# Seven block products instead of eight for five column pairs of the second token half in an input projection

## The chip, the cores and the metric

The kernel runs as one program on one core of a Trainium2 chip. The metric is device time in microseconds (us), the median over runs; before the change three runs gave 2535.07, 2537.70 and 2538.64 us, median 2537.7. The engines are named as in the profile: PE does the matrix products (a "matmul" is one instruction with up to 512 moving columns), DVE elementwise work on vectors, ACT elementwise functions and copies, POOL small elementwise work and DMAs of its own queue; SP issues most DMAs. A *bank* is one 128x512 fp32 accumulator of PE.

## The reference

One layer over T = 2048 tokens with D = 1024 features, all in fp32: token mixing, cross-attention into 256 memory tokens, and a gated feed-forward net, each between two RMS norms. The part around the change is token mixing:

```python
u = rms_norm(h, g_mix_pre[l])
z = u @ w_in[l]                      # (2048 x 1024) @ (1024 x 2816)
qa, ka, va, qh, fh, ih, gh = jnp.split(z, IN_SPLITS, axis=-1)
ya = swa_with_sinks(qa, ka, va, sinks[l])     # 8 query heads, 2 key heads, chunk-banded
yh = hgrn2(qh, fh, ih, gh, lb, onorm)         # 4 heads of a gated recurrence
y = concat([ya, yh]) @ w_out[l]
h = h + rms_norm(y, g_mix_post[l])
```

The 2816 columns of z are 22 columns of 128, numbered 0 to 21: 0 to 3 are attention's queries, 4 its keys, 5 its values, 6 to 9 the recurrence's queries, 10 to 13 its forget gates f, 14 to 17 its inputs, 18 to 21 its output gates.

## The kernel before, in words

**Products.** fp32 is emulated: each operand is split into a high part (`hi`, written by ACT or POOL) and a low part (`lo` = raw − hi, written by DVE, line 1038), and each product is three matmuls, hi·hi, hi·lo and lo·hi (`mm3`, lines 156 to 158, for plain products; `products`, lines 1198 to 1200, for block products).

**Block products.** Large products are cut into 2x2 blocks on both operands. A step with four results needs eight block products plainly, or seven with sums of operands and of results (the Winograd form; `seven`, in the order 1, 5, 6, 3, 7, 2, 4). The operand that stays is called T (tokens; T[1], T[8], T[2], T[3] are raw blocks, T[5], T[7], T[6], T[4] sums), the one that is loaded per step S (weights; `streamed`). For the input projection one step is a pair of columns for 1024 tokens: each block product is 12 matmuls of 128x512, so 84 in seven products and 96 plainly. The results leave the banks by ACT copies (`part`, line 1213) and by `out`, which adds on DVE and then applies what the column needs: a split into halves for columns 0 to 4, a copy, or a tanh with a product. For a pair with an f column, `after` runs `decays`: Ln on ACT, two cumulative scans on DVE (line 794), exponentials.

**Two token halves.** `in_first` handles tokens 0 to 1023 for all 11 pairs (`ORDER`: (4,5), (0,1), (2,3), (10,6), (11,7), (12,8), (13,9), (14,15) to (20,21)). Pairs 0 and 1 start in plain forms while the first tokens come in, the others are steps in seven products. `phases` plans them: it has a list of steps, knows at which step each T tile is used first and last, and forms a T tile (`resident`: ACT high part, DVE low part, in two halves) when a slot's last user is past. There are 7 slots. Then `in_first` splits the second half's four raw token blocks into `u` tiles and does the first pair of the second half plainly, 96 matmuls.

**Columns as filler.** The other 20 columns of the second half are done one at a time by `in_cols`: two token blocks of 24 matmuls each into a `psg` bank, with weights split by POOL or ACT (`whi`) and DVE (`wlo`). `in_proj` is a generator, and `mix` takes one column from it at given places between the steps of attention: one ahead, one after each of the first 9 rounds (a round is one step of `swa` and one of `hgrn`), one after each of the 8 remaining steps of `swa`, and two around the first step of `fold` (the cross-attention's preparation).

**An attention step.** `swa` works by blocks of 128 tokens. `swa_front(n)` loads queries and keys, makes scores on PE (128x256, lines 859 and 860), reduces and exponentiates them (line 864 on DVE with a read of its accumulator, line 868 on ACT), makes the softmax's denominators with small operations on POOL and ACT (lines 871 to 874) and scales (line 879 on DVE). `swa_back(n)` transposes on PE (line 893), splits into `pth` (ACT, line 897) and `ptl` (DVE, line 898), multiplies by the values (lines 902 and 903) and writes the result to `ys` by ACT (line 904), once for each of two key heads. `ys` has one buffer. It holds a high and a low partial result in two halves of its partitions: SP stores the first half into `y_d` in DRAM, and POOL's DMA adds the second half to the same place (line 907):

```python
ys = ph.tile([P, 2, 512], F32, tag="ys", name=f"ys{n}")
...
self.store(dst, ys[0:64])
nc.gpsimd.dma_start(dst, ys[64:128], accum_op=ALU.add)
```

`hgrn_front` loads k, q, v, multiplies k and q by decays on POOL (lines 931, 943, 946) and makes products on PE. The order on every engine is fixed when the program is built: a scheduler places the instructions of the generators by its own estimate of time, so a column need not stand where `mix` took it.

Of the kernel before, what the change touches and what calls it, by code (L numbers as in the profile page):

```python
# [18 lines left out]
P = 128  # L19
T = 2048  # L20
# [28 lines left out]
class Layer:  # L49
# [146 lines left out]
    def mix(self):  # L196
        tc, I = self.tc, self.I
        kw = dict(reuse_waits="tile")
        with contextlib.ExitStack() as left:
# [18 lines left out]
            with tc.tile_pool(name="sw", bufs=1, side="right", **kw) as self.sw:  # L218
# [5 lines left out]
                for _ in range(NPB + 1):  # L224
                    next(swa)
                    next(hgrn)
                    next(cols)
# [207 lines left out]

    ORDER = [(4, 5), (0, 1), (2, 3)] + [(10 + h, 6 + h) for h in range(4)] + [(c, c + 1) for c in range(14, 22, 2)]
# [31 lines left out]
    def in_first(self):  # L468
# [63 lines left out]
        second = {}  # L532

        def fetch():
            for s in range(2):
                for q in range(2):
                    r = self.pair_tile().rearrange("p a d -> p (a d)")
                    self.load(r.rearrange("p (n c) -> p n c", n=4),
                              self.un_d[4 * s:4 * s + 4, q].rearrange("n p c -> p n c"))
                    second[q, s] = r.rearrange("p (m k c) -> p k m c", m=16, k=4)  # L540
                    yield

        beside = [(), (0,), (1, 2), (3,), (4,), (5,), (6,), (7,), (), (), (), ()]
        get = fetch()
        tokens = [[] for _ in range(len(self.ORDER) + 1)]
        blocks = [("s",) + self.in_block(*p, tokens[i], tokens[i + 1], beside[i + 1], get if i > 9 else (), i < 2,
                                         None if i else lambda: x_loads(0, (2, 3)))
                  for i, p in enumerate(self.ORDER)]

# [3 lines left out]
        phases = self.phases([(lambda i, j, a, n: raw[i, j][:, a:a + n, :], 4, blocks, None, {})], T)  # L553
# [46 lines left out]
        for _ in get:  # L600
            pass
        u = []
        for s in range(2):
            u.append([])
            for q in range(2):
# [18 lines left out]
        for s in range(2):  # L624
# [1238 lines left out]
```

## Time and profile before

| | |
|---|---|
| runs | 2535.07, 2537.70, 2538.64 us; median 2537.7 |
| profiled execution | 2533.9 us, of which the span 2532.2 us |
| PE | busy 2493.8 us of the span (98%) |
| DVE, ACT, POOL | busy 1749.1, 1240.7 and 365.4 us |
| first token half and first pair of the second | about 0 to 280 us |
| attention steps with columns | about 285 to 616 us |
| cross-attention, feed-forward | from there to the end |

In the groups of the profile a line reads: source line, engine, operation, what it writes and reads, shape, count, then busy time, mean ns of one, and the idle time just before these instructions with what released most of it. In the timelines a row reads start, duration, engine, line, operation, and in brackets the idle time before it with its releaser. A busy PE includes overlap of neighbouring matmuls.

### The profile page before, as it was taken

The numbers are of one execution on the slowest core, as the hardware profiler recorded it, in microseconds if no ns is written. First come the engines' busy times: TensorE is split into PE (matmuls) and PEld (weight loads), VectorE is DVE, ScalarE is ACT, GpSimd is POOL, SyncE is SP. The second block draws the span as 40 slices with busy tenths as digits, with TensorE's granted clock in tenths as the row PEclk, the third lists the DMA queues.
The fourth block names the chain that finished last, engine by engine and source line by source line (L and its number), as shares of the span: only waits on it lengthen the run. The fifth ranks groups of instructions, "written<-read, shape, count | busy, mean of one in ns | idle before, by whom it ended". The sixth has DMA issues, their size and how long they took to land.

```text
span 2532.2 us, 33939 instructions
## 1 busy us (share of the span) xinstructions
PE 2493.8 (98%) x11942; PEld 2084.7 (82%) x11942; DVE 1749.1 (69%) x2787; ACT 1240.7 (49%) x2582; POOL 365.4 (14%) x540
## 2 busy tenths in 40 slices
PE   9999999999999999999999999999999999999998
PEld 8778888888987788878878888888888888888886
DVE  8896477865556989988866655576566557574766
ACT  5463356654565576566753333353333335443543
POOL 4241244321400111112200000000000000000122
PEclk9999999999999999999999999999999999999999
DMA  7544877785887996858944322254354334565777
GB/s 221 158 158 164 239 198 178 223 270 135 278 298 266 302 335 194 255 175 255 339 164 169 136 76 93 78 196 154 129 208 167 117 127 156 177 184 110 231 169 156
DMA packets 313403, 483.56 MB, mean 191 GB/s; under 512 B 21904, under 2 KB 198032, under 8 KB 313232
## 3 DMA queue, kind: packets, MB, share of 16 engines
q1 hardware_dynamic: 304880, 455.17, 54.1%
q0 software_dynamic: 8352, 26.22, 6.1%
q8 instruction: 94, 1.54, 0.2%
q14 instruction: 77, 0.63, 0.1%
HBM read 305.15 MB, written 176.16 MB: 190 GB/s over the span
## 4 chain that ended last, share of the span: by engine, by line
PE 83%; DVE 5%; DMA 5%; issue 2%; ACT 2%; POOL 1%; SPq 1%; DVEq 0%; POOLq 0%; ACTq 0%
PE psm L1200 22%; PE psm L1198 22%; PE psm L1199 22%; PE psg L158 2%; PE psg L156 2%; PE psg L157 2%; DVE S L1038 1%; DMA y_d<-ys 1%; DVE T L1038 1%; DMA raw<-in_wo_x_dram 1%; DVE sum L1173 0%; DMA pair<-in_x_dram 0%; DMA out_s<-u 0%; SPq L75 0%; ACT junk L1569 0%
## 5 line engine op out<-in xcount | busy, mean ns | idle before, releaser
L1198 PE MATMUL psm<-T,S 128*128 128x512 f32 x2680 | 1034.4, 391 | 12.6 <-ACT part L1213 8.4
L1199 PE MATMUL psm<-T,S 128*128 128x512 f32 x2680 | 1042.6, 390 | 1.2 <-DVE T L1038 1.1
L1200 PE MATMUL psm<-T,S 128*128 128x512 f32 x2680 | 1030.0, 390 | 5.0 <-DVE S L1038 5.0
L1198 PEld LDWEIGHTS psm<-T,S 128*128 128x128 f32 x2680 | 503.1, 188 | 124.8 <-ACT part L1213 13.0
L1200 PEld LDWEIGHTS psm<-T,S 128*128 128x128 f32 x2680 | 503.4, 188 | 112.4 <-DVE S L1038 8.4
L1199 PEld LDWEIGHTS psm<-T,S 128*128 128x128 f32 x2680 | 503.5, 188 | 106.7 <-DVE T L1038 3.0
L1035 ACT ACTIVATE S<-sum 128x512 fp32r<-128x512 f32 (+1 forms) x370 | 224.1, 619 | 374.8 <-PE psm L1200 270.4
L1038 DVE TENSOR_TENSOR S<-sraw,S 128x512 fp32r<-128x512 f32 (+1 forms) x315 | 212.0, 679 | 236.9 <-ACT S L1035 233.7
L1213 ACT ACTIVATE part<-psm 128x512 f32<-128x512 f32 x285 | 168.6, 596 | 253.1 <-PE psm L1200 237.8
L1038 DVE TENSOR_TENSOR S<-sum,S 128x512 fp32r<-128x512 f32 (+1 forms) x388 | 258.0, 673 | 43.9 <-ACT S L1035 40.0
L1035 ACT ACTIVATE S<-sraw 128x512 fp32r<-128x512 f32 (+1 forms) x300 | 184.5, 618 | 110.7 <-PE psm L1200 108.7
L1602 POOL DMA_DIRECT2D y_d<-row x16 | 14.0, 872 | 1077.3 <-DVE row L1784 1015.3
L1038 DVE TENSOR_TENSOR T<-row,T 128x1024 fp32r<-128x1024 f32 (+1 forms) x112 | 130.8, 1183 | 28.3 <-ACT T L1035 26.4
L156 PE MATMUL psg<-u,whi 128*128 128x512 f32 x320 | 127.6, 399 | 0.7 <-DVE z L770 0.5
L157 PE MATMUL psg<-u,whi 128*128 128x512 f32 x320 | 127.3, 398 | 0.0
L158 PE MATMUL psg<-u,wlo 128*128 128x512 f32 x320 | 126.7, 397 | 0.0
L1569 ACT ACTIVATE junk<-row 128x512 f32<-128x512 f32 x160 | 99.6, 624 | 46.3 <-DVE row L1591 19.9
L1035 ACT ACTIVATE T<-row 128x1024 fp32r<-128x1024 f32 (+1 forms) x112 | 113.4, 1031 | 10.6 <-DMA row<-d_s 5.3
L1735 DVE TENSOR_TENSOR row<-psm,part 128x512 f32<-128x512 f32 x66 | 44.0, 687 | 71.3 <-PE psm L1200 71.3
L1038 DVE TENSOR_TENSOR wlo<-raw,whi 128x1024 fp32r<-128x1024 f32 x52 | 65.4, 1258 | 36.0 <-ACT whi L1035 30.9
L1784 DVE TENSOR_TENSOR row<-psm,part 128x512 f32<-128x512 f32 x72 | 49.1, 687 | 49.3 <-PE psm L1200 49.2
L1744 DVE TENSOR_TENSOR part<-psm,part 128x512 f32<-128x512 f32 x66 | 43.7, 687 | 52.2 <-PE psm L1200 52.2
(355 smaller groups left out, 3476.2 us busy)
## 6 DMA issues: line engine op xcount, KB each, us to landing
sraw<-in_w_gate_dram SPq DMA_DIRECT2D x44, 512.0 KB, 3.8
sraw<-in_w_up_dram SPq DMA_DIRECT2D x44, 512.0 KB, 3.6
hid_d<-row SPq DMA_DIRECT2D x44, 512.0 KB, 2.6
sraw<-hid_d SPq DMA_DIRECT2D x32, 512.0 KB, 4.6
sraw<-in_w_in_dram SPq DMA_DIRECT2D x48, 256.0 KB, 3.9
raw<-in_w_in_dram SPq DMA_DIRECT2D x20, 512.0 KB, 6.3
row<-in_w_down_dram SPq DMA_DIRECT2D x20, 512.0 KB, 7.3
row<-d_s SPq DMA_DIRECT2D x20, 512.0 KB, 8.4
```

The lines of the kernel that those rows point to most:

```text
L156: nc.tensor.matmul(ps, ah, bh, start=(i == 0), stop=False)
L157: nc.tensor.matmul(ps, ah, bl, start=False, stop=False)
L158: nc.tensor.matmul(ps, al, bh, start=False, stop=(i == n - 1))
L1035: self.nc.scalar.activation(hi, raw, AF.Copy)
L1038: self.nc.vector.tensor_tensor(lo, raw, f32(hi), ALU.subtract)
L1198: nc.tensor.matmul(ps, s[:, 0, k, :], t[:, 0, k, :], start=st, stop=False, **kw)
L1199: nc.tensor.matmul(ps, s[:, 0, k, :], t[:, 1, k, :], start=False, stop=False, **kw)
L1200: nc.tensor.matmul(ps, s[:, 1, k, :], t[:, 0, k, :], start=False, stop=sp, **kw)
L1213: nc.scalar.activation(t, ps, AF.Copy)
L1569: self.nc.scalar.activation(junk, a, AF.Square, scale=float(D) ** -0.5, accum_out=to)
L1735: nc.vector.tensor_tensor(d, a, c, ALU.add)
L1784: nc.vector.tensor_tensor(d, a, b, ALU.add)
```

## The change

The second half's first five pairs, (4,5), (0,1), (2,3), (10,6) and (11,7), become steps in seven products as well, as a second job in `phases`. Twelve columns are left for `in_proj`.

- `sums` loads the four raw token blocks of the second half and makes in place, on DVE, what T[7], T[5] and T[6] need, in six operations of 128x1024; T[4] is a difference of two of these, made on the way. T[3]'s block and, at the third pair, T[8]'s block are loaded again.
- The second job's T tiles take the slots of the first job's tiles of the same number (`where`), each when its last user is past.
- The four `u` tiles and the plain pair go. Of the second job's T tiles, T[1], T[2] and T[3] serve the columns, and T[8] is split anew.
- `in_block` takes the token half as an argument; its two-scan `decays` now runs for two pairs of the second half there instead of in `in_cols`.
- `mix` takes columns at 12 places: one ahead, one after rounds 1, 3, 5 and 7, one after each remaining step of `swa` but two, and one at `fold`.

```diff
-                for _ in range(NPB + 1):
+                for i in range(NPB + 1):
                     next(swa)
                     next(hgrn)
-                    next(cols)
+                    if i in (1, 3, 5, 7):
+                        next(cols)
...
-                    next(cols)
+                    if i not in (11, 14):
+                        next(cols)
...
+    MORE = 5
...
+        more = [("s",) + self.in_block(*p, 1, (), [], (), False, None) for p in self.ORDER[:self.MORE]]
+        second = {}
+
+        def fetched(q, s):
+            r = self.pair_tile().rearrange("p a d -> p (a d)")
+            self.load(r.rearrange("p (n c) -> p n c", n=4),
+                      self.un_d[4 * s:4 * s + 4, q].rearrange("n p c -> p n c"))
+            return r.rearrange("p (m k c) -> p k m c", m=16, k=4)
+
+        def sums():
+            for k, at in ((7, (1, 1)), (5, (0, 1)), (1, (0, 0)), (2, (1, 0))):
+                second[k] = fetched(*at)
+                yield
+            for d, a, b, op in ((7, 7, 5, ALU.subtract), (5, 5, 1, ALU.subtract), (6, 1, 7, ALU.add)):
+                if d == 6:
+                    second[6] = self.pair_tile().rearrange("p a d -> p (a d)").rearrange("p (m k c) -> p k m c",
+                                                                                         m=16, k=4)
+                for k in (0, 2):
+                    kk = slice(k, k + 2)
+                    nc.vector.tensor_tensor(second[d][:, kk], second[a][:, kk], second[b][:, kk], op)
+                    yield
+
+        def operand(i, j, a, n):
+            key = i if j is None else {(0, 0): 1, (1, 0): 2, (1, 1): 3}[i, j]
+            if key == 3 and not a:
+                second[3] = fetched(1, 1)
+            if key == 4:
+                return second[2][:, a:a + n], second[6][:, a:a + n]
+            return second[key][:, a:a + n]
+
+        def again():
+            second[8] = fetched(0, 1)
+            yield
...
+        phases = self.phases([(lambda i, j, a, n: raw[i, j][:, a:a + n, :], 4, blocks, None, {len(blocks) - 2: [sums]}),
+                              (operand, 4, more, True, {2: [again]})], T)
...
-        u = []
-        for s in range(2):
-            u.append([])
-            for q in range(2):
-                self._n += 1
-                t = self.big.tile([P, 2, 4, 512], F32R, tag="big", name=f"u1_{q}{s}")
-                r = second[q, s]
-                for k in (0, 2):
-                    self.split2(r[:, k:k + 2], *(t[:, e, k:k + 2].rearrange("p k (m c) -> p k m c", m=16)
+        T[8] = self.big.tile([P, 2, 4, 512], F32R, tag="big", name="u1_01")
+        for k in (0, 2):
+            self.split2(second[8][:, k:k + 2], *(T[8][:, e, k:k + 2].rearrange("p k (m c) -> p k m c", m=16)
                                                  for e in range(2)), "A")
-                u[s] += [(t[:, 0, k, :], t[:, 1, k, :]) for k in range(4)]
-
-        c0 = self.ORDER[0][0] * P
-
-        def load(t, j):
-            for i, c in enumerate(self.ORDER[0]):
-                self.load(t[:, :, i * P:(i + 1) * P], I["w_in"][c, :, 4 * j:4 * j + 4, :])
-
-        stream = self.streamed(load, 4, "p")
-        next(stream)
-        S = list(stream)
-        z, low = self.pair_tile(), self.pair_tile()
-        for s in range(2):
-            sl = slice(s * 512, (s + 1) * 512)
-            for i in range(2):
-                ps = self.bank("g")
-                self.mm3(ps, [((S[i + k // 4 * 2][:, 0, k % 4, :], S[i + k // 4 * 2][:, 1, k % 4, :]), u[s][k])
-                              for k in range(KT)])
-                if i:
-                    nc.scalar.activation(z[:, i, sl], ps, AF.Copy)
-                else:
-                    self.halves(c0, ps, z[:, 0, sl], low[:, 0, sl])
-        self.store_halves(c0, TB, z[:, 0, :], low[:, 0, :])
-        self.store(self.z_d[c0 + P:c0 + 2 * P, TB:2 * TB], z[:, 1, :])
-        return u
+        for p in (1, 2, 3):
+            T[p] = T[1, p, 0]
+        return [[(T[p][:, 0, k, :], T[p][:, 1, k, :]) for p in ps for k in range(4)] for ps in ((1, 2), (8, 3))]
...
-        for c in order[2:]:
+        for c in order[2 * self.MORE:]:
...
+                if first and queue[0][0]:
+                    free = next(s for s in slots if s[2] == where[queue[0][1]])
```

How the built program differs at three places. Names carry a running number; an "x2" means two such instructions in a row. Line numbers behind the change are 2 to 7 lower.

PE late in the attention stage. Before, in the middle of one step (`psh` and `vst` are products with the values, `psg` with `whi` and `wlo` a column):

```order
L156 MATMUL psg_6266<-u_00_2232,whi_6261 128x512
L902 MATMUL psh_5937<-pth_10_5924,vst_5427 128x512
L157 MATMUL psg_6266<-u_00_2232,whi_6261 128x512
L158 MATMUL psg_6266<-u_00_2232,wlo_6262 128x512
L156 MATMUL psg_6266<-u_10_2237,whi_6261 128x512
L157 MATMUL psg_6266<-u_10_2237,whi_6261 128x512
L158 MATMUL psg_6266<-u_10_2237,wlo_6262 128x512
L156 MATMUL psg_6266<-u_10_2237,whi_6261 128x512
L903 MATMUL psh_5937<-ptl_10_5925,vst_5427 128x512
L902 MATMUL psh_5937<-pth_11_5933,vst_5626 128x512
```

After, at the corresponding stretch (`pss` and `pst` on `ident` are the transposes of the probabilities):

```order
L896 MATMUL psh_5776<-ptl_11_5773,vst_5467 128x512
L886 MATMUL pst_5942<-ident,S_00_5669 128x128 x2
L886 MATMUL pst_5942<-ident,S_01_5679 128x128 x2
L886 MATMUL pss_5933<-ident,S_00_5669 128x128 x2
L886 MATMUL pss_5933<-ident,S_01_5679 128x128 x2
L895 MATMUL psh_5951<-pth_00_5938,vst_5467 128x512
L886 MATMUL pss_5957<-ident,S_10_5702 128x128 x2
L886 MATMUL pss_5957<-ident,S_11_5712 128x128 x2
L886 MATMUL pst_5966<-ident,S_10_5702 128x128 x2
L886 MATMUL pst_5966<-ident,S_11_5712 128x128 x2
L896 MATMUL psh_5951<-ptl_00_5939,vst_5467 128x512
L895 MATMUL psh_5951<-pth_01_5947,vst_5664 128x512
```

The column's matmuls are gone from between the products with the values. Behind the eleventh of the twelve columns, 208 rows in a row, from the last of `psg_6472` to the first of `psg_6554`, hold no column's matmul; before, the longest such run is 23 rows. Counted with repeats, the 208 rows hold 125 matmuls of 128x128, 80 of 128x256, 56 of 128x512 and 4 of 128x192.

POOL at the end of these steps. `y_d<-ys` is the adding DMA, `w_se` and `w_dn` are the denominators of later steps, `k` is what PE's last product ahead of the twelfth column reads. Before:

```order
L907 DMA y_d<-ys_5695 64x2x512
L871 TENSOR_TENSOR w_se_5883<-sink,w_mn_5861 128x4
L874 TENSOR_TENSOR w_dn_5886<-w_den_5862,w_se_5883 128x4
L1037 TENSOR_SCALAR whi_6370<-raw_6368 128x1024
L871 TENSOR_TENSOR w_se_6047<-sink,w_mn_6025 128x4
L874 TENSOR_TENSOR w_dn_6050<-w_den_6026,w_se_6047 128x4
L907 DMA y_d<-ys_5894 64x2x512
L871 TENSOR_TENSOR w_se_6080<-sink,w_mn_6058 128x4
L874 TENSOR_TENSOR w_dn_6083<-w_den_6059,w_se_6080 128x4
L946 TENSOR_TENSOR k_6321<-k_6321,G_563 128x4x64
L907 DMA y_d<-ys_6091 64x2x512
```

After:

```order
L900 DMA y_d<-ys_5932 64x2x512
L864 TENSOR_TENSOR w_se_6060<-sink,w_mn_6038 128x4
L867 TENSOR_TENSOR w_dn_6030<-w_den_6006,w_se_6027 128x4
L867 TENSOR_TENSOR w_dn_6063<-w_den_6039,w_se_6060 128x4
L864 TENSOR_TENSOR w_se_6226<-sink,w_mn_6204 128x4
L900 DMA y_d<-ys_6071 64x2x512
L864 TENSOR_TENSOR w_se_6259<-sink,w_mn_6237 128x4
L867 TENSOR_TENSOR w_dn_6229<-w_den_6205,w_se_6226 128x4
L867 TENSOR_TENSOR w_dn_6262<-w_den_6238,w_se_6259 128x4
L900 DMA y_d<-ys_6270 64x2x512
L939 TENSOR_TENSOR k_6500<-k_6500,G_563 128x4x64
```

The splits `whi` of the columns' weights are gone from between, and `k` now stands directly behind the adding DMA of the last of these steps instead of ahead of it.

DVE where attention begins. `pair` here is the f pair's result and its scans, `wlo` the low part of a column's weights. Before:

```order
L1038 TENSOR_TENSOR S_2267<-sraw_2255,S_2267 128x512
L1038 TENSOR_TENSOR u_11_2247<-pair_2230,u_11_2247 128x1024 x2
L707 SCALAR_TENSOR_TENSOR pair_2169<-th_2190,pair_2169 128x512
L707 SCALAR_TENSOR_TENSOR pair_2169<-th_2210,pair_2169 128x512
L707 SCALAR_TENSOR_TENSOR pair_2169<-th_2225,psm_2096 128x512
L642 SCALAR_TENSOR_TENSOR pair_2271<-psm_2272,pair_2270 128x512
L1038 TENSOR_TENSOR wlo_2419<-raw_2416,whi_2418 128x1024
L1038 TENSOR_TENSOR wlo_2599<-raw_2596,whi_2598 128x1024
```

After:

```order
L687 TENSOR_TENSOR pair_2948<-psm_2867,part_2902 128x512
L807 SCALAR_TENSOR_TENSOR pair_2802<-pair_2802,pair_2887 128x1024
L687 TENSOR_TENSOR pair_2948<-psm_2984,part_2880 128x512
L700 SCALAR_TENSOR_TENSOR pair_2948<-th_2972,pair_2948 128x512
L700 SCALAR_TENSOR_TENSOR pair_2948<-th_3012,psm_2867 128x512
L787 SCALAR_TENSOR_TENSOR pair_3015<-reset,pair_3015 128x512 x2
L1031 TENSOR_TENSOR wlo_3078<-raw_3075,whi_3077 128x1024
L793 TENSOR_TENSOR pair_3015<-pair_3015,d_mid_3019 128x1024
```

Ahead of the first column's `wlo` there now stand the last f pair's sums and products and two scans (`pair_3015<-reset,pair_3015`).

More of the change, by code (lines that the diff above doesn't have):

```diff
@@ L648, in store_halves, with in_block @@
             self.store(dst[e, r:r + P, t0:t0 + t.shape[1]], t)
-    def in_block(self, ca, cb, x, ahead, beside, get, plain, between):
+    def in_block(self, ca, cb, b, x, ahead, beside, plain, between):
         nc, w = self.nc, self.I["w_in"]
@@ L662, in stream, with out @@
         def stream(kind):
-            for _ in range(3):
-                next(iter(get), None)
             return self.streamed(load, 4, kind)
-        def out(i, j, a, b):
+        def out(i, j, a, o):
             c0 = (ca, cb)[i] * P
@@ L1062, in split @@
         def split(a, b, t, o):
+            if type(t) is tuple:
+                t, o = t
             if o is not None:
                 nc.vector.tensor_tensor(t, t, o, ALU.add if key == 6 else ALU.subtract)
[L1065 removed]
+            hi, lo = dst[:, 0, a:b], dst[:, 1, a:b]
+            if len(t.shape) == 4:
+                hi, lo = (x.rearrange("p k (m c) -> p k m c", m=16) for x in (hi, lo))
+            self.split2(t, hi, lo, "A")
         src = []
@@ L1302, in phases @@
         held = 7 if first else -1
-        slots = [("A", -2, i) for i in range(4)] + [("B", held if i == 2 else -1, i) for i in range(3)]
-        T, keep = {}, [{} for _ in jobs]
+        slots = [("A", -2, i) for i in range(4)] + [("B", held if i == 6 else -1, i) for i in range(4, 7)]
+        T, keep, where = {}, [{} for _ in jobs], {}
         current, left = [None], {}
@@ L1313, in phases @@
                 slots[i] = ("A", uses[k][-1], i)
+                where[p] = i
         def fetch(n, tile):
@@ L1346, in half @@
                 n, p, _ = k = queue.pop(0)
+                where[p] = free[2]
                 slots.remove(free)
@@ L1353, in half @@
                 T[k] = dst
+                if first:
+                    first[k] = dst
                 left[k] = 2
```

34 lines of the change are left out of this document (10 added, 24 removed).

## Prediction

> **What bounds the kernel now.** I read the page first, then busy time by stages, then PE's timeline inside the stages, and last the rows of `ys`, the buffer that ends an attention step.
>
> ```profile
> span 2532.2 us, 33939 instructions
> PE 2493.8 (98%) x11942; PEld 2084.7 (82%) x11942; DVE 1749.1 (69%) x2787; ACT 1240.7 (49%) x2582; POOL 365.4 (14%) x540
> ```
>
> The 98% is an average, so the stage around the change is read by itself: from 285 to 500 us attention steps alternate with the second half's columns.
>
> ```profile
> core 0: us, PE busy (x) PEld busy (x) DVE busy (x) ACT busy (x) POOL busy (x), PEclk, DMA share, GB/s
> 285.00:500.00 215.00, 214.81 (x1260) 187.50 (x1259) 153.52 (x398) 129.70 (x397) 79.22 (x128) 1.00 0.73 201
> ```
>
> PE never rests here (214.81 of 215); DVE is at 71% (153.52). The 0.39 us of a matmul overlaps its neighbours', so I price PE's work by the distance of starts.
>
> ```profile
> 179.75 0.39 PE L1199 MATMUL psm<-u,S 128*128 128x512 f32 x1
> ...
> 191.99 0.39 PE L1199 MATMUL psm<-T,S 128*128 128x512 f32 x1
> ```
>
> ```profile
> 584.48 0.28 PE L859 MATMUL pss<-kk,qs 128*128 128x256 f32 x1
> ...
> 585.32 0.28 PE L860 MATMUL pst<-kk,qs 128*128 128x256 f32 x1
> ...
> 593.42 0.60 PE L893 MATMUL pss<-ident,S 128*128 128x128 f32 x4
> 593.86 0.49 PE L893 MATMUL pst<-ident,S 128*128 128x128 f32 x3
> ```
>
> 54 starts in 12.24 us make 0.227 us for 512 columns, 7 in 0.84 make 0.12 for 256, 4 in 0.44 make 0.11 for 128. So PE's work bounds the time now, as long as each attention step brings enough of it.
>
> **The change part by part: products.** A pair done plainly takes 96 matmuls of 128x512, in seven products 84; a single column takes 48. Before, the second half has 96 + 20×48 = 1056; after, 5×84 + 12×48 = 996. The built program has 60 fewer such matmuls, so the change does what it says: 60 × 0.227 = **−13.6 us**, if PE stays as full.
>
> **What the columns covered.** Of the 20 single columns taken among the attention steps 12 stay. In the order of PE (front section, first pair of pieces) the twelve don't stand spread: the scheduler has drawn eleven ahead, and behind the eleventh comes a stretch of about five attention steps with not one matmul of a column. Counted there: 125 matmuls of 128x128, 80 of 128x256, 56 of 128x512, 4 of 128x192. PE's work in it: 125×0.11 + 80×0.12 + 56×0.227 + about 0.7 = 36.7 us. Now what the other engines need for the same stretch, with durations from this stage:
>
> ```profile
> L879 DVE TENSOR_SCALAR S<-S,w_rd 128x256 f32<-128x256 f32 x120 | 39.8, 394 | 1.9
> L864 DVE CUSTOM_DVE_ANT_0 S<-pst,wmask,nsink 128x256 f32<-128x256 f32 x60 | 26.6, 477 | 1.6 <-PE pst L860 1.6
> L864 DVE DVE_READ_ACCUMULATOR2_ANT w_mn<- 128x1 f32 x124 | 10.1, 81 | 0.0
> L898 DVE TENSOR_TENSOR ptl<-pss,pth 128x512 fp32r<-128x512 f32 x32 | 21.9, 683 | 4.0 <-ACT pth L897 3.9
> L1038 DVE TENSOR_TENSOR wlo<-raw,whi 128x1024 fp32r<-128x1024 f32 x17 | 21.4, 1261 | 3.5 <-POOL whi L1037 3.4
> ```
>
> By the order DVE does there 40 score operations with 40 reads (40 × 0.558 = 22.3 us), 44 scalings (44 × 39.8/120 = 14.6), 28 `ptl` (19.1), one `wlo` (1.3) and some 20 small ones (about 4, my estimate): 61 us. So the stretch can't be shorter than about 61, and PE idles at least 61 − 37 = 24 us in it. That is the low end.
>
> The high end comes from the store of the step's result. `ys` has one buffer. ACT writes it twice, SP stores it, POOL adds it into the same place of y_d and must wait for that store to land, and only when POOL's DMA has landed may ACT write the next `ys`; ACT's later work stands behind.
>
> ```profile
> 563.05 0.60 ACT L904 ACTIVATE ys<-psh 128x512 f32<-128x512 f32 x1 [1.30 <-PE psg L158]
> ...
> 580.57 0.60 ACT L904 ACTIVATE ys<-psh 128x512 f32<-128x512 f32 x1 [1.43 <-PE psg L158]
> ...
> 595.13 0.60 ACT L904 ACTIVATE ys<-psh 128x512 f32<-128x512 f32 x1 [0.41 <-PE psh L903]
> ...
> 599.11 0.61 ACT L904 ACTIVATE ys<-psh 128x512 f32<-128x512 f32 x1
> ...
> 611.60 1.09 ACT L904 ACTIVATE ys<-psh 128x512 f32<-128x512 f32 x2 [6.98 <-DMA y_d<-ys]
> ```
>
> ```profile
> 600.31 0.58 SPq L78 DMA_DIRECT2D y_d<-ys  x1
> ```
>
> ```profile
> 606.11 0.98 POOL L907 DMA_DIRECT2D y_d<-ys  x1 [3.48 <-DMA y_d<-ys]
> ```
>
> The second write ended at 599.72 and the next began at 611.60: 11.9 us, 6.98 of them with ACT idle although the matmuls were done. Here a column covers this; in the new stretch nothing does. A round is then the 11.9 plus the two writes back to back, 1.09: 13.0 us. The rounds that the rows show are 17.5, 14.6 and 16.5 us (mean 16.2), but with columns on PE's path. I take 13.0 and keep 16.2 for the high end. The stretch: the write before it is fed by products some 20 matmuls (about 4.5 us) ahead of its start, so the buffer comes free 11.9 − 4.5, about 7 us in; six first writes lie in it, so five rounds, 65 us; and at its end PE waits for POOL's product `k`, which by POOL's order (second pair of pieces) stands directly behind the last accumulation: 1.09 + 0.59 to the store, 5.80 to POOL, 0.98, and some 0.6 for the product, 9 us. In all 7 + 65 + 9 = 81 us, PE idle 81 − 37 = **+44 us** (24 to 60, the latter with 16.2 a round). POOL's wait for the store also holds up the small denominators queued behind it, for which ACT and then DVE wait; that is why I go by the ring and not by DVE's sum.
>
> **Into the attention stage.** Before, the columns' first `wlo` stood on DVE behind the split of the new operands. After, two scans of the last decay stand ahead of it (third pair of pieces), and these hang on a chain from the f pair's last product: sum, tanh, POOL, a table load, Ln, two scans, `wlo`.
>
> ```profile
> L702 POOL TENSOR_SCALAR pair<-pair,fb,fa 128x512 f32<-128x512 f32 x8 | 14.1, 1765 | 8.7 <-ACT pair L700 6.3 <-ACT G L808 2.4
> L790 ACT ACT_TABLE_LOAD x4 | 5.1, 1283 | 0.1
> L700 ACT ACTIVATE pair<-pair 128x512 f32<-128x512 f32 x8 | 5.0, 628 | 12.2 <-DVE pair L694 12.2
> L790 ACT ACTIVATE pair<-pair 128x1024 f32<-128x1024 f32 x4 | 4.2, 1062 | 4.3 <-POOL pair L702 4.3
> L794 DVE TENSOR_TENSOR_SCAN u<-reset,x 128x512 f32<-128x512 f32 x8 | 9.4, 1210 | 2.5 <-ACT x L790 2.5
> ```
>
> With the sum at `ptl`'s size, 0.68 + 0.63 + 1.77 + 1.28 + 1.06 + 2×1.21 + 1.26 = 9.1 us, against which PE holds the last product's 12 matmuls, four of the column and four small ones: 4.3. **+5 us** (0, if a scan slips behind, to 8). An f pair also stalls in itself:
>
> ```profile
> 109.49 0.39 PE L1200 MATMUL psm<-T,S 128*128 128x512 f32 x1
> 113.02 0.50 PE L1198 MATMUL psm<-T,S 128*128 128x512 f32 x1 [3.15 <-ACT part L1213]
> ...
> 116.34 0.63 PE L1199 MATMUL psm<-T,S 128*128 128x512 f32 x1
> 116.77 0.63 PE L1200 MATMUL psm<-T,S 128*128 128x512 f32 x1
> ```
>
> This is the worst of the four; the other three lose about 1 us each. Two more come with the second half: **+1 us** (0 to 5).
>
> **New operands.** Between the two sets DVE makes six sums, two for a seventh operand and fourteen halves of T, 22 × 1.2 (a 128x1024 operation, by `wlo`) = 27 us on top of its product work, over the five pairs' 420 × 0.227 = 95 us, most of it in their first 75. Blocks of this form load it as the first stretch shows:
>
> ```profile
> 0.00:250.00 250.00, 238.12 (x1127) 197.97 (x1128) 199.25 (x267) 126.93 (x205) 77.54 (x109) 0.99 0.55 175
> ```
>
> DVE is at 80% already (199.25 of 250); 27 us in 75 is more than the fifth that is free. But the T tiles are made one product ahead where a slot is free, which hides part: **+2 us** (0 to 8). The first four attention steps, where DVE's sum is 66 us to PE's 63 by the same counting, **+2** (0 to 6). Operand loads, stores of z and the split of one tile instead of four are hidden behind DMA queues at 55 to 75%, or were on DVE before too: 0.
>
> Sum: −13.6 + 44 + 5 + 1 + 2 + 2 = +40.4. The profiled execution took 2533.9 us, so 2574.3; it lies 3.8 below the median of the runs (2537.7), and I say 2575. About 0.2%, 5 us, is what a measurement of this kernel can tell from no change.
>
> **The rivals.** *The ring doesn't decide, DVE's work does.* Against it stand the 6.98 us of ACT's idle time in the quoted round; for it, that a round of 13.0 isn't far over DVE's 61/5 = 12.2, and that the entries may be hidden. Idle 24: −13.6 + 24 + about 8 gives +18, **2552**, down to 2545 when all small terms are nought. 0.22.
>
> *Faster: attention keeps up.* If the steps of the stretch flow into the stage before it, DVE and ACT working ahead while PE still runs columns, the stretch costs PE no more than its own work and the loss of products shows: −13.6 + 5 = −9, **2525**. It decides where the stretch takes less than 36.7 + 13.6 = 50 us. DVE's 61 us speaks against it, and so does `ys`, which lets ACT no more than one step ahead; for it speaks DVE's 71% in the stage before, which leaves room for work ahead. 0.07; a draw between it and the last rival 0.03.
>
> *PE slows in the gaps.* After the 3.15 us of idle time above, the starts are 0.43 us apart (116.34 to 116.77), twice the usual. Gaps of 4 to 8 us come in each round of the stretch, and then its 37 us of matmuls could take up to twice as long. They lie on the round's path only between scores and `ys`, some 2 to 3 us each: five or six rounds × 2.7 = 16, **2591**. 0.13. The Trainium skill, "TensorE: Matmul & The Clock Gate", section "Part 1: The HAM clock gate (the "warmup" mystery)", says that the array falls to half its clock after an idle window of some 3.4 us and regains it only after a like window of work; the 0.43 us behind 3.15 idle agrees, and by that rule every round here would go at half rate.
>
> **How the numbers follow.** Ring 0.55, DVE 0.22, slow PE 0.13, faster 0.07, draw 0.03. The time is the ring's. The range reaches from the DVE case with small terms (2548) to the ring at 15 us a round or the slow PE with the small terms at their upper ends (2598); beyond it lie the faster case and the draw, 0.10, the low end of the DVE case, 0.05, and the slowest of the slow PE, 0.05: 0.2 together. Slower is 0.55 + 0.22 + 0.13 = 0.90, and 0.02 of it I give to the draw and the faster case for what I can't see of work ahead: 0.88, 0.04, 0.08.
>
> **What would show it.** In the new profile: ten or eleven columns at about 98% PE, then a stretch near 80 us with PE busy under half, ACT's `ys` idle before with y_d<-ys as releaser in five or six rounds some 13 us apart, then `psg<-ident,k` released by POOL. DVE idle inside the rounds shows the ring, DVE full shows the first rival; starts 0.43 us apart show the third. Wrong would be a stretch under 50 us, or idle time that lies in the five new pairs instead.

## The result and the profile after

The changed kernel takes 2569.68 us (median of four runs, 2568.08 to 2574.71), the kernel before beside it 2536.51. The ratio is 1.0133, interval [1.0116, 1.0151]: slower by 33 us. The forecast was 2575 in a range of 2548 to 2598. The profiled execution took 2568.08 us, 34.2 more than that of before.

First the top of the page of the kernel after, then busy time by stages around the change (the first line of the view names its fields).

```profile
span 2566.4 us, 33991 instructions
PE 2500.7 (97%) x11882; PEld 2082.6 (81%) x11882; DVE 1800.3 (70%) x2861; ACT 1266.9 (49%) x2623; POOL 367.8 (14%) x544
```

```profile
core 0: us, PE busy (x) PEld busy (x) DVE busy (x) ACT busy (x) POOL busy (x), PEclk, DMA share, GB/s
250.00:345.00 95.00, 93.26 (x408) 76.06 (x407) 70.56 (x96) 43.52 (x67) 13.84 (x20) 1.00 0.35 124
345.00:575.00 230.00, 218.94 (x1242) 188.34 (x1242) 160.93 (x404) 125.62 (x388) 91.34 (x138) 0.96 0.85 243
582.00:649.60 67.60, 48.82 (x269) 37.77 (x268) 51.27 (x178) 46.40 (x148) 12.25 (x31) 0.92 0.57 128
```

PE has exactly 60 matmuls fewer (11942 to 11882), and is newly idle in two places: 11 us between 345 and 575, and 19 us in the stretch without columns, where its granted clock is 0.92 of the full one, so that some of the busy time is slow work. The new pairs, up to 345 us, run nearly full.

The stretch begins behind the eleventh column's last matmul (581.81) and ends where the twelfth's first starts, 649.64: 67.8 us.

```profile
581.81 0.40 PE L158 MATMUL psg<-T,wlo 128*128 128x512 f32 x1
...
649.22 0.66 PE L942 MATMUL psg<-ident,k 128*128 128x128 f32 x4 [1.19 <-POOL k L939]
649.64 0.47 PE L156 MATMUL psg<-T,whi 128*128 128x512 f32 x1
```

ACT's writes of `ys` in it, three of its rounds:

```profile
587.22 0.60 ACT L897 ACTIVATE ys<-psh 128x512 f32<-128x512 f32 x1 [0.16 <-issue]
589.84 0.60 ACT L897 ACTIVATE ys<-psh 128x512 f32<-128x512 f32 x1 [0.67 <-PE psh L896]
599.41 0.60 ACT L897 ACTIVATE ys<-psh 128x512 f32<-128x512 f32 x1 [2.85 <-DMA y_d<-ys]
602.12 0.60 ACT L897 ACTIVATE ys<-psh 128x512 f32<-128x512 f32 x1 [0.97 <-PE psh L896]
611.71 0.60 ACT L897 ACTIVATE ys<-psh 128x512 f32<-128x512 f32 x1 [2.16 <-issue]
...
622.60 0.60 ACT L897 ACTIVATE ys<-psh 128x512 f32<-128x512 f32 x1 [2.59 <-issue]
```

Rounds are 12.2, 12.3 and 10.9 us; up to the sixth first write at 641.93 five rounds take 54.7, 10.9 on average. ACT idles before each first write. The rows name the landing of y_d<-ys, "issue" (something that the profile doesn't name) or, at 631.48 and 641.93, a matmul, but in every round the write starts within 0.1 us of the landing of POOL's adding DMA. The second write of a round can wait for PE as well (0.67 and 0.97 us in the rows); in the shortest round, 8.9 us from 622.60 to 631.48, it follows the first at once. The end of the stretch is POOL's, as the order had it:

```profile
647.54 0.98 POOL L900 DMA_DIRECT2D y_d<-ys  x1 [8.00 <-ACT atz L933]
648.21 0.96 POOL L939 TENSOR_TENSOR k<-k,G 128x256 f32<-128x256 f32 x1
```

The entry, on PE, on POOL and on SP:

```profile
345.26 0.39 PE L1198 MATMUL psm<-T,S 128*128 128x512 f32 x1
350.80 0.80 PE L156 MATMUL psg<-T,whi 128*128 128x512 f32 x1 [5.15 <-POOL whi L1030]
351.39 0.63 PE L157 MATMUL psg<-T,whi 128*128 128x512 f32 x1
351.82 0.63 PE L156 MATMUL psg<-u,whi 128*128 128x512 f32 x1
```

```profile
349.01 1.73 POOL L1030 TENSOR_SCALAR whi<-raw 128x1024 fp32r<-128x1024 f32 x1 [0.70 <-DMA raw<-in_w_in_dram]
```

```profile
341.74 2.30 SPq L78 DMA_DIRECT2D z_d<-pair  x2
344.13 0.38 SPq L75 DMA_DIRECT2D raw<-in_w_in_dram  x1
```

The stall has the forecast size, 5.15 us, and another cause: the weights' load was issued at 344.13, behind two stores of an f pair for which SP had waited, and PE waited for load and split (`whi`), not for the scans. And a stall that nobody forecast, with its cause on DVE:

```profile
448.29 0.79 PE L896 MATMUL pst<-ptl,vst 128*128 128x512 f32 x1 [3.91 <-DVE ptl L891]
448.88 0.63 PE L895 MATMUL pst<-pth,vst 128*128 128x512 f32 x1
449.31 0.41 PE L852 MATMUL pst<-kk,qs 128*128 128x256 f32 x1
```

```profile
446.41 1.23 DVE L1080 TENSOR_TENSOR u<-u,x 128x1024 f32<-128x1024 f32 x1 [4.59 <-DMA out_s<-u]
447.55 0.69 DVE L891 TENSOR_TENSOR ptl<-pst,pth 128x512 fp32r<-128x512 f32 x1
```

DVE stood 4.59 us in a sum of output weights that waited for a DMA, and `ptl`, for which PE waited, was queued behind it.

### The profile page after: what moved, and what is told of

The parts are those of the page before. It is cut to its first block, busy times and chain, and to the rows that moved or that the text cites. A ratio compares the mean times of both kernels' runs of the same rounds, so it can differ in the third digit from the quotient of the medians.

```text
span 2566.4 us, 33991 instructions
## 1 busy us (share of the span) xinstructions
PE 2500.7 (97%) x11882; PEld 2082.6 (81%) x11882; DVE 1800.3 (70%) x2861; ACT 1266.9 (49%) x2623; POOL 367.8 (14%) x544
## 4 chain that ended last, share of the span: by engine, by line
PE 77%; DVE 7%; DMA 7%; ACT 3%; issue 3%; POOL 1%; SPq 0%; DVEq 0%; POOLq 0%; ACTq 0%
PE psm L1196 22%; PE psm L1198 22%; PE psm L1197 22%; PE psg L158 1%; PE psg L156 1%; PE psg L157 1%; DVE S L1031 1%; DMA y_d<-ys 1%; DMA pair<-in_x_dram 1%; DVE T L1031 1%; DMA y_d<-sg 1%; DMA raw<-in_wo_x_dram 1%; ACT junk L1573 1%; DMA h1t_d<-row 1%; DVE row L1628 1%
## 5 line engine op out<-in xcount | busy, mean ns | idle before, releaser
L1196 PE MATMUL psm<-T,S 128*128 128x512 f32 x2820 | 1088.7, 391 | 15.8 <-ACT part L1211 10.7
L1197 PE MATMUL psm<-T,S 128*128 128x512 f32 x2820 | 1097.1, 390 | 1.3 <-DVE T L1031 1.1
L1198 PE MATMUL psm<-T,S 128*128 128x512 f32 x2820 | 1084.1, 390 | 3.4 <-DVE S L1031 3.4
L1196 PEld LDWEIGHTS psm<-T,S 128*128 128x128 f32 x2820 | 530.0, 188 | 135.0 <-ACT part L1211 16.2
L1198 PEld LDWEIGHTS psm<-T,S 128*128 128x128 f32 x2820 | 530.0, 188 | 116.9 <-DVE S L1031 6.8
L1197 PEld LDWEIGHTS psm<-T,S 128*128 128x128 f32 x2820 | 530.3, 188 | 112.4 <-DVE T L1031 3.3
L1028 ACT ACTIVATE S<-sum 128x512 fp32r<-128x512 f32 (+1 forms) x380 | 230.0, 620 | 384.0 <-PE psm L1198 280.9
L1031 DVE TENSOR_TENSOR S<-sraw,S 128x512 fp32r<-128x512 f32 (+1 forms) x326 | 220.1, 681 | 238.3 <-ACT S L1028 236.2
L1211 ACT ACTIVATE part<-psm 128x512 f32<-128x512 f32 x300 | 177.6, 596 | 267.5 <-PE psm L1198 251.3
L1031 DVE TENSOR_TENSOR S<-sum,S 128x512 fp32r<-128x512 f32 (+1 forms) x408 | 271.7, 675 | 45.5 <-ACT S L1028 40.9
L1171 DVE TENSOR_TENSOR sum<-sraw,sraw 128x512 f32<-128x512 f32 (+1 forms) x102 | 71.1, 697 | 16.6 <-DMA sraw<-in_w_in_dram 11.7
L1031 DVE TENSOR_TENSOR wlo<-raw,whi 128x1024 fp32r<-128x1024 f32 x44 | 54.6, 1241 | 32.7 <-ACT whi L1028 28.8
L861 ACT ACTIVATE S<-S,w_mn 128x256 f32<-128x256 f32 (+1 forms) x128 | 63.1, 497 | 21.6 <-DVE w_mn L857 21.4
L1584 POOL TENSOR_TENSOR q_v<-q_s 128x2 f32<-128x2 f32 x39 | 14.3, 366 | 414.8 <-ACT junk L1573 414.8
```

What stands on the lines that cost most here:

```text
L861: nc.scalar.activation(s[:, r, o:], s[:, r, o:], AF.Exp, bias=mn[:, i:i + 1], scale=-1.0, accum_out=den[:, i:i + 1])
L1028: self.nc.scalar.activation(hi, raw, AF.Copy)
L1031: self.nc.vector.tensor_tensor(lo, raw, f32(hi), ALU.subtract)
L1171: nc.vector.tensor_tensor(t, a, b, op)
L1196: nc.tensor.matmul(ps, s[:, 0, k, :], t[:, 0, k, :], start=st, stop=False, **kw)
L1197: nc.tensor.matmul(ps, s[:, 0, k, :], t[:, 1, k, :], start=False, stop=False, **kw)
```

## The experiments

The theory after the result: attention steps without columns run at the pace of `ys`'s ring, since the change took columns away (*cover*). Its rivals: other engines' work sets that pace, or the price lies in what the change adds. Times are medians, ratios are against the kernel before on the same chip; "less" and "more" are against the changed kernel's 2569.68.

**Two buffers for `ys`**, in the changed kernel and in the one before:

```diff
-        ys = ph.tile([P, 2, 512], F32, tag="ys", name=f"ys{n}")
+        ys = ph.tile([P, 2, 512], F32, tag="ys", name=f"ys{n}", bufs=2)
```

> The changed kernel with two buffers for ys, so that a step's result can be written while the one before it is still being stored and added. Ring theory: in the stretch without columns (581.9 to 649.6 us, rounds of 8.9 to 12.3 us, mean 10.9) each first write of ys began 0.07 us after the landing of the adding DMA, so without that wait a round falls to DVE's work, 8.4 us (50.3 us busy in six rounds), or a bit over: six rounds by 1 to 2.4 us, 2556 to 2564 us. Rival, the chain through scores, exponentials, denominators and products sets the pace and the ring only happens to end last: 2566 to 2574 us, and ACT waits for PE where it waited for the DMA.

> The kernel before with two buffers for ys, as a control. Both theories: PE is covered by columns there and the ring costs nothing, 2531 to 2541 us. If it is faster by more than 5 us, the ring cost time before the change too and the base of the comparison has to be thought over.

After: 2562.68, ratio 1.0096 [1.0079, 1.0113], 7.0 less. Before: 2534.49, 0.9989 [0.9980, 0.9999], 3.2 less than the kernel before, at most a trace faster. In the changed kernel with two buffers the stretch runs from 581.89 to 645.25, 63.4 us instead of 67.8. Its ends, its windows, and ACT in it:

```profile
581.89 0.39 PE L158 MATMUL psg<-T,wlo 128*128 128x512 f32 x1
...
645.25 0.47 PE L156 MATMUL psg<-T,whi 128*128 128x512 f32 x1
```

```profile
582.00:644.00 62.00, 48.59 (x271) 38.10 (x269) 49.54 (x171) 45.71 (x144) 10.00 (x29) 0.92 0.60 135
```

```profile
599.45 0.60 ACT L897 ACTIVATE ys<-psh 128x512 f32<-128x512 f32 x1 [3.13 <-PE psh L896]
...
605.61 0.59 ACT L897 ACTIVATE ys<-psh 128x512 f32<-128x512 f32 x1
```

No write waits for a DMA any more, ACT now waits for PE, and DVE is at 80%. The ring is confirmed as the wait that ended last in a round, and its price is only 4.4 us of the stretch. By the prediction's count PE's work in it takes 36.7 us at the full clock, so that 31 of the 67.8 us are lost (19 us idle, the rest in matmuls at a lower clock or without a neighbour to overlap). The other 27 us stay without the ring: DVE's work and the chain from engine to engine stood close behind. What the run gains beyond these 4.4 us lies outside the stretch; where, is not shown.

**Columns spread by halves.** Each half column's matmuls are held behind the attention step that `mix` had built last:

```diff
+                with self.queued(*self.hold):
+                    self.mm3(ps, [...])
...
+                    self.hold = (self.traced(mybir.EngineType.PE),)
+                    for _ in range([1, 2, 1, 2, 1, 2, 1, 2, 1][i]):
+                        next(cols)
```

> The changed kernel with the matmuls of the twelve columns held back by halves: a half column (24 matmuls, 5.4 us) or two behind each attention step, none ahead of its step, so that no stretch is longer than 10 us of PE work without one. Cover theory: the 30 us of idle time of the stretch go for the most part, and what stays is the stall at the entry (about 10 with its half-rate matmuls) and some new gaps between blocks: 2535 to 2553 us. Rival, the time was lost to what the change adds (sums, T tiles, f pairs, the entry) and not to missing cover: over 2560 us.

2592.94, ratio 1.0219 [1.0204, 1.0234]: 23 more. The cover theory's range is missed. The rival's bound is met, but not for its reason, since the time that is lost on top is lost in attention steps and not in the five pairs.

```profile
346.00:500.00 154.00, 131.46 (x701) 111.90 (x700) 104.67 (x263) 81.21 (x248) 62.86 (x95) 0.89 0.86 248
```

Now the early steps leave PE idle for 22 us of 154. In the trace the half columns lie as blocks of 24 and of 48 matmuls by turns, 5.4 and 10.9 us, with PE idle between them, mostly for DVE. I read it so that a full step doesn't lend its cover to the next; no run tests this alone.

**Columns spread by quarters**, with twelve matmuls held behind marks inside the steps, so that they lie between groups of attention's matmuls; then with two buffers for `ys`, and with that and the store queue of the next experiment:

```diff
+                for q in range(2):
+                    with self.queued(*self.hold[q]):
+                        self.mm3(ps, pairs[4 * q:4 * q + 4], not q, q)
...
+                    self.hold = tuple(self.marks[-6:][:1] if q == 0 else self.marks[-4:][:1] for q in range(2))
```

> The changed kernel with the columns held back by quarters (12 matmuls each, 2.7 us), so that they lie between the single groups of each attention step: every step has 5 to 11 us of column matmuls, and the longest run without is 5.8 us. One buffer for ys. Cover theory, in the form that the first spread leaves (steps with and without a column in turn don't average out, each step needs its own): the stretch's 30 us of idle time go to under 12, the entry's 10 stay: 2540 to 2553 us. Rival, holding columns back costs what it gains, as in the first spread: over 2565 us.

> The same spread with two buffers for ys. PE's work per late step is about 11.0 us with its half column, DVE's 8.4 to 9.5, the ring's round was 10.9: the ring is at the point of deciding, so two buffers gain 1 to 6 us on the run with one: 2537 to 2550 us.

> The same spread with two buffers for ys and the f pair's stores by ACT's queue. The two effects are at different places and add: the gain of after_store_queue on top of the run before it, by the queue theory 7 to 10 us (2530 to 2541), by the chain theory 0 to 3.

2571.29, 2560.81 and 2559.66 (ratios 1.0127 [1.0112, 1.0143], 1.0092 [1.0077, 1.0107], 1.0090 [1.0073, 1.0106]). The spread gains nothing: with one buffer 2 more than the changed kernel, with two 2 less than that with two. All three times lie above those of the cover theory, and the first is the rival's case: holding back costs what it gains. Two buffers took off 10 us here, more than the 1 to 6 that were expected, and the store queue 1.2 more, its lower case. The run with two buffers shows why:

```profile
347.00:575.00 228.00, 209.69 (x1200) 180.03 (x1199) 163.76 (x427) 130.08 (x410) 92.41 (x141) 0.95 0.85 238
575.00:652.00 77.00, 71.43 (x392) 58.93 (x391) 53.80 (x172) 48.39 (x141) 13.73 (x30) 0.98 0.58 144
```

Late, PE's idle time fell to 6 us of 77. Early it rose from 11 to 18 us. The columns were brought to where they lacked and now lack where they were.

**The store queue at the entry.** The f pair's two stores go by ACT's queue:

```diff
-                    self.store(self.z_d[c * P:(c + 1) * P, b * TB:(b + 1) * TB], z[0][:, i, :])
+                    (self.nc.scalar if b and ca == 10 else self.nc.sync).dma_start(
+                        self.z_d[c * P:(c + 1) * P, b * TB:(b + 1) * TB], z[0][:, i, :])
```

> The changed kernel with the two stores of the first f pair of the second half sent by ACT's queue instead of SP's, where they held up the load of the first column's weights (PE waited 5.15 us for POOL's whi, which waited for that load). PE's order is unchanged. If the prediction's chain is next behind it (tanh, POOL, table load, Ln, two scans, wlo, done at 352.9 us), the first matmuls come earlier but PE then waits for wlo: gain 0 to 3 us, 2567 to 2571. If the queue was all of the entry's cost, the stall of 5.3 and the matmuls at half rate behind it go: gain 7 to 10 us, 2560 to 2563.

2571.24, ratio 1.0129 [1.0113, 1.0144]: no gain, so the queue was not all. Nor was the next wait for the scans and `wlo`, as the chain theory had it:

```profile
343.67 0.39 PE L1199 MATMUL psm<-T,S 128*128 128x512 f32 x1
347.79 0.50 PE L156 MATMUL psg<-T,whi 128*128 128x512 f32 x1 [3.73 <-POOL whi L1031]
...
351.74 1.65 PE L932 MATMUL psh<-qq,k 128*128 128x192 f32 x4 [2.74 <-POOL qq L925]
```

The wait for the weights is shorter by 1.4 us, and one for the recurrence's first operand, loaded by SP right after them, takes its place.

**The first column's weights ahead**, loaded and split two pairs earlier, with five pair tiles in place of six to make room:

```diff
+            hi, lo = (self.mc.tile([P, D], F32R, name=f"ahead{i}") for i in range(2))
+            t = self.pair_tile()[:, 0, :]
+            self.load(t, I["w_in"][c].rearrange("p k c -> p (k c)"))
+            self.split(t, hi, lo, "P")
```

> The changed kernel with the first column's weights loaded and split two pairs earlier, into tiles of their own (room for them: five pair tiles in place of six). Entry theory: PE has a whole column, 48 matmuls or 10.9 us, ready when the last product ends, so the 5.3 us of waiting and the matmuls at half rate behind it go: 2560 to 2564 us. Shortage theory: attention's first step starts no earlier, so a column spent at the entry is missing at the end, where PE's work without columns grows from 36.7 to 39.9 us by the order; the idle time moves there in part: 2564 to 2569 us. Rival, with five pair tiles the blocks themselves wait: 2570 us or more, with new idle time before 345 us.

2578.02, ratio 1.0167 [1.0149, 1.0185]: 8 more.

```profile
352.08 0.39 PE L1204 MATMUL psm<-T,S 128*128 128x512 f32 x1
352.31 0.39 PE L156 MATMUL psg<-T,ahead 128*128 128x512 f32 x1
...
367.45 0.47 PE L156 MATMUL psg<-T,whi 128*128 128x512 f32 x1 [2.80 <-ACT z L764]
...
379.98 0.30 PE L858 MATMUL pst<-kk,qs 128*128 128x128 f32 x1 [2.95 <-DMA kk<-zk_d]
...
655.00 0.48 PE L156 MATMUL psg<-T,whi 128*128 128x512 f32 x1
```

The stall is gone, from the last product to the column without a gap. But the last product comes at 352.08 instead of 345.26, 6.8 us later, with 3.5 us of new waits for halves of T at 256 to 262 us; the run doesn't separate the missing tile from the added load and split. And from there to the twelfth column's first matmul (655.00) it is 302.9 us, against 304.4 in the changed kernel (345.26 to 649.64): of the entry's stall 1.5 us came back, the rest stands as other waits behind it. The stretch without columns at the end grew from 67.8 to 76.5 us. This is the shortage theory's case, on top of the rival's.

**Twenty columns again**, with the last eight computed twice and columns taken at all the places of the kernel before:

```diff
-        for c in order[2 * self.MORE:]:
+        for c in order[2 * self.MORE:] + order[14:]:
```

> The changed kernel with as many columns as before: the last eight of the twelve are computed twice, into the same rows, and columns are taken at all the places of the kernel before. Against the kernel before it has 420 block matmuls in place of the first pair's 96, 324 x 0.227 = 73.5 us more work of PE. Cover theory: with 20 columns no stretch lacks cover, so what is left over 73.5 is the price of the five new pairs and of the entry alone, about 10: 2616 to 2626 us, and the eight columns cost 50 us in place of 87. Rival, the change's other work slows the attention stage too: over 2635, up to 2657 (2569.7 + 87).

2621.04, ratio 1.0336 [1.0312, 1.0361], in the cover theory's range, and the rival's is missed.

```profile
500.00:646.00 146.00, 146.00 (x829) 125.53 (x829) 93.24 (x279) 79.54 (x251) 37.42 (x64) 1.00 0.64 170
```

PE is busy without a break where the changed kernel has its hole. The eight columns are 8 × 48 × 0.227 = 87.2 us of work and cost 51.4. Against the kernel before (2535.81) the run takes 85.2 more, of which 73.5 are block products: 11.7 are left for all else that the change adds, the entry first, where PE waits 6.27 us for `whi` in this run.

**Three pairs instead of five**, with sixteen columns taken at sixteen places: as the scheduler lays them, then spread by quarters with two buffers for `ys`, then with the last pair's stores by ACT's queue.

```diff
-    MORE = 5
+    MORE = 3
```

> The changed kernel with three pairs of the second half in seven products (the three without an f column) and sixteen columns left, taken at one place ahead, six of nine rounds, all eight later steps and fold. Products: 36 fewer matmuls than before, -8.2 us. Cover theory: PE's work without columns at the end of attention falls from 36.7 to 19.9 us, so its idle time falls from 30 to about 12 to 16, the entry without an f pair costs 2 to 5: 2541 to 2553 us. Rival, the loss comes with the f pairs and the entry alone: 2525 to 2535 us.

> Three pairs in seven products, sixteen columns held back by quarters (11 us of column matmuls in each of the first ten steps, 5 to 11 in the later ones), two buffers for ys. Shortage theory, from the five-pair spread: a step needs some 9 us of column matmuls for PE not to wait, 16 steps 150 us; twelve columns bring 131, sixteen 174. So the idle time at the end of attention (19 us in after_three_pairs) goes and the entry's 10 stays: 2537 to 2546 us. Rival, holding columns back makes as much idle time elsewhere, as with five pairs: 2555 to 2563.

> The same with the last pair's four stores by ACT's queue, so that the first column's weights are not behind them on SP. By after_store_queue's result the next wait is close behind (k and q of the first recurrence step, loaded by the same queue after the weights): 0 to 4 us less than three_pairs_spread. If the entry here hangs on that queue alone, 7 to 10 us less.

2560.40, 2552.38 and 2551.80 (ratios 1.0086 [1.0071, 1.0101], 1.0064 [1.0044, 1.0084], 1.0059 [1.0041, 1.0076]). The first is above both ranges, the second between those of its two theories, the third, 0.6 less, within the lower case. Without an f pair the entry is no shorter:

```profile
314.53 0.79 PE L156 MATMUL psg<-T,whi 128*128 128x512 f32 x1 [6.40 <-POOL whi L1030]
```

The f pair's chain is thus not what the entry costs. That stall, over the 2 to 5 us that were forecast for the entry, and 11.5 us of idle time between 600 and 650 us are why the first run missed both ranges. The second run is 8 us faster than the first; two buffers alone took 7.0 with five pairs, so that no gain of the spread itself is shown. And where the "9 us a step" of the shortage theory should have left only the entry, 8 us of idle time stay between 475 and 600 us:

```profile
475.00:600.00 125.00, 117.28 (x639) 97.51 (x638) 85.55 (x240) 66.87 (x212) 31.79 (x55) 0.97 0.81 238
```

No version with the new pairs comes nearer to the kernel before than 0.6%.

## Why the prediction was right, point by point

The direction, the time and the place of the loss were right. The reason for its size was for the most part not: "the time is the ring's", but without the ring the kernel is still 25 us slower than before. That the total came so near is in part luck, since errors cancel.

By the experiments the change is −13.6 for the products, +11.7 for what it adds at full cover (the twenty columns), and 87.2 − 51.4 = 35.8 for the cover of eight columns. Both prices come from the one run with twenty columns, so their sum meets the measured 33.2 by construction; what the run shows is how it divides. The profile of the changed kernel gives a second account: −13.6, 31 in the stretch, 9 at the entry and 7 at 448 us, 33 together. The prediction had −13.6, 44, 5 and 5: the stretch 13 too dear, the rest 6 too cheap.

**Products, −13.6.** The 60 matmuls are gone, and the run with twenty columns came within its forecast with this price of a matmul.

**The stretch, +44.** It came 67.8 us long instead of 81, and 67.8 − 36.7 = 31 of it are lost. By the terms of the sum, 5.4 + 54.7 + 7.7 for 7 + 65 + 9. No column, a ring that ends each round and POOL's `k` at the end are in the rows; the size of a round was wrong, 10.9 for 13.0. The price was taken from one round under columns and heavy traffic. The view of DMAs shows, from issue to landing in the stages 500 to 616 us before and 582 to 650 us after:

```profile
y_d<-ys POOLq DMA_DIRECT2D x7, 256.0 KB, 7.0
y_d<-ys SPq DMA_DIRECT2D x7, 256.0 KB, 4.9
```

```profile
y_d<-ys POOLq DMA_DIRECT2D x7, 256.0 KB, 4.6
y_d<-ys SPq DMA_DIRECT2D x6, 256.0 KB, 3.2
```

Both legs are shorter, by 2.4 and 1.7 us, with the DMA share at 0.57 instead of 0.75. That the removed columns had loaded the queue which was priced fits this; no run separates it. 13.0 less these 4.1 is 8.9, the shortest round; in the others the second write waited for PE's product, which the term of 13.0 had back to back. The step that failed is the choice to "go by the ring and not by DVE's sum": the ring ended last, but two buffers took only 4.4 us from the stretch.

**DVE's sum as the low end, 24.** It rested on 61 us, but DVE's busy time in the stretch is 51.3. Its instructions overlap too, as PE's were priced and DVE's were not:

```profile
600.02 0.47 DVE L857 CUSTOM_DVE_ANT_0 S<-psh,wmask,nsink 128x256 f32<-128x256 f32 x1
600.42 0.08 DVE L857 DVE_READ_ACCUMULATOR2_ANT w_mn<- 128x1 f32 x1
600.42 0.48 DVE L857 CUSTOM_DVE_ANT_0 S<-psh,wmask,nsink 128x256 f32<-128x256 f32 x1
```

A score operation with its read takes 0.40 us from start to start (the run with two buffers), not 0.558. So by busy time DVE alone would have left about 15 us; the ring adds about 4 by the run, and the other 12 or so are the chain between engines and matmuls at a lower clock, not taken apart here.

**Into attention, +5.** 5.15 us, but by the weights' load and split. The step that failed is "two scans of the last decay stand ahead of it": they do, and `wlo` was done only at 352.93, but SP's queue and POOL's `whi` held PE, and neither here nor in the run with the store queue did PE wait for `wlo`. So the size is luck. A second wait of 0.76 us and the matmuls behind the stall, 0.43 us apart, come on top: about 9 us in all.

**f pairs, +1, operands, +2.** No stall over 1 us in the five pairs (PE 93.26 of 95): both came out near nothing, DVE's load was hidden. **Early steps, +2.** PE waits 1.6 us in all between 351 and 444 us, mostly for a transfer (0.58) and POOL (0.76), not for DVE's sum. What cost more there, about 7 us, is the stall that ends at 448.29 with its slow matmuls, which no term had.

**The rivals.** DVE alone: by its busy time about half of what the stretch lost; no run tests it alone. Faster: the stretch would have had to be under 50 us, it was 67.8. The slow clock is real, but smaller than forecast:

```profile
599.40:611.70 12.30, 8.79 (x45) 6.99 (x45) 9.52 (x35) 8.00 (x27) 1.77 (x5) 0.86 0.58 134
611.70:622.60 10.90, 7.79 (x46) 5.97 (x46) 8.29 (x31) 7.89 (x27) 1.81 (x5) 1.00 0.68 151
622.60:631.50 8.90, 7.04 (x27) 5.45 (x28) 6.49 (x24) 6.45 (x22) 1.87 (x5) 0.62 0.34 61
```

Two of these three rounds were granted less than the full clock, and the slowest clock stands in the shortest round: so it didn't set the length of a round. The rival had counted on gaps of 4 to 8 us in each round; the longest idle time of PE in the stretch is 3.16 us. The granted clock is 0.50 for 10.2 us of the stretch (600.68 to 604.09 and 624.57 to 631.40), so that it cost 5 us at most by this count, not 16, and not every round went at half rate. What the experiments corrected is the word *cover* itself. I had thought of a hole at the end that could be filled; the spreads show that the stage as a whole has too few columns, and that filling one place opens another.

## What to carry to other kernels

Work that an engine in fixed order does between the steps of a long chain saves less than its own time when it is taken away: here eight columns are 87 us of work and cost only 51 when they were put back. Before such filler is cut, ask what the stage would take without it, and price that with durations from start to start on every engine, and with transfers as they are without the filler's own load. Moving the rest of the filler about did not help here, where the sum is short; find that out with one run before tuning its places. And a wait that ends last need not be worth much: two buffers took the ring's wait away and little time, since the next wait stood close behind.

## What the runs showed of the hardware

Behind idle times of 5.15 and 3.91 us PE's matmuls start 0.43 us apart, twice the usual 0.227, and at the second place this lasts from 448.29 to about 454 us. The granted clock is 0.50 there from 447.08 to 453.90 us, 6.8 us, and from 348.09 to 358.33, 10.2 us, at the entry. The Trainium skill, "TensorE: Matmul & The Clock Gate", section "Part 1: The HAM clock gate (the "warmup" mystery)", tells of a window of about 3.4 us for both ways, which runs freely, so that the slow time differs from run to run. The traces agree: between the start and the end of the program the slow times are 3.4, 6.8 or 10.2 us in every run here, one to three times 3.41. The 6.8 us at the second place began within the idle time.

Two things go beyond that. The slow time need not start with the first matmul behind a wait, and no idle time as long as the window is needed. Behind the 3.73 us in the run with the store queue the first matmuls still start 0.23 us apart, and the clock falls at 348.85, 1.1 us after work had begun again. In the changed kernel it falls at 624.57, where PE was busy for 1.56 of the 3.41 us before and the longest idle time in them was 1.71 us.
